# A new order of all operations in a two-layer attention and MLP kernel on one core

## The chip, the cores and the metric

The kernel runs on 1 core of one Trainium2 chip. The metric is the time of one execution on the device, in microseconds (us). The core has five engines with an instruction queue each: TensorE (PE; its weight loads are listed as PEld), VectorE (DVE), ScalarE (ACT), GpSimd (POOL) and SyncE (SP, which here only issues DMAs). Each engine works through its own queue in order; between engines, semaphores make an instruction wait for its inputs and for its buffers.

## The reference

A causal decoder trunk of two layers on 256 tokens of width 1024, in float32. Layer 0 mixes tokens with block-sparse attention of 16 heads, whose one block of 256 tokens covers the sequence, layer 1 with a dilated sliding-window attention of 12 heads in three groups. Each mixer is followed by an MLP of width 4096 with a squared ReLU, and each of the four parts by a layer norm:

```python
for i in range(DEPTH):                                   # DEPTH = 2
    mix = moba_attention(h, ...) if i % 2 == 0 else dilated_attention(h, ...)
    h = layer_norm(DEEPNORM_ALPHA * h + mix, ln_mix_g[i], ln_mix_b[i])
    h = layer_norm(DEEPNORM_ALPHA * h + sq_relu_mlp(h, w_in[i], w_out[i]), ...)

def sq_relu_mlp(x, w_in, w_out):
    return jnp.square(jax.nn.relu(x @ w_in)) @ w_out
```

## The kernel before

The function `tile_trunk` does not issue instructions as it goes. It records 3550 operations in a `Plan`: each with its engine, the function that issues it, and the operations that must come before it because of what it reads and writes. Then `Plan.emit` issues them in the order that the table `ORDER` (from line 236) gives. `ORDER` holds differences: its running sums are the numbers of the operations. Every engine's queue is that one list, cut down to the engine's own operations; so the table sets the order on TensorE, VectorE, ScalarE, POOL and SP all at once.

```python
ops = [self.ops[n] for n in itertools.accumulate(ORDER)]
```

The buffers rotate: tiles of one tag (`raw` 8 of them, `whi` 9, `wlo` 10, `ta` 6, and four PSUM banks each for `tp` and `acc`) are handed out in the order of the list, the one that came free first going first. A tile's first operation waits for the last operation on the tile that had the place before it. So a new order also changes which tile follows which.

The products are done with float32 numbers split into two parts: `split` makes the upper part on ScalarE (L433, `whi<-raw`) and the remainder on VectorE (L438, `wlo<-raw,whi`), and TensorE multiplies the parts (L443, three matmuls for one product). Weights come by DMA in pieces of 512 KB, issued on SP (`load_w`). Activations are transposed on TensorE by a product with the identity (L945).

The MLP's second product uses a scheme with seven block products instead of eight, for which sums of weight blocks are needed. `load_left` and `load_right` (L720 to L760) load two tiles and form these sums. Some are done by `add_by_dma` (L706): two accumulating DMAs of half a tile each, issued on POOL (L712). Each takes one of the three tiles named `ring`, so that a fourth has to wait until the one three before it has landed; and each waits for the `split` of the tile it adds to, whose VectorE part is the last to be done. Since POOL's queue is in order, what stands behind a waiting half waits too. The sum is then read by a VectorE add of two tiles in `raw` (L804, `raw<-raw,raw`) and by the next `split`.

In the MLP's first product, the two halves of a PSUM bank are added by `halves_sum`: ScalarE copies one half out of the bank (L1185) and VectorE adds the other to it (L804, `ta<-tp,ta`). That add is the last reader of the bank and gives it back to TensorE.

The operation numbers that the prediction speaks of:

- 2812 and 2817: the VectorE part of the splits that gate the halves of the tiles raw_952 (2813, 2814) and raw_957 (2818, 2819); 2835: the VectorE add that reads raw_952's sum.
- 1177 and 1182: the same for raw_385 (1178, 1179) and raw_388 (1183, 1184); 1241: the VectorE add that reads raw_385's sum.

Of the kernel before, what the change touches and what calls it, by code (L numbers as in the profile page):

```python
# [136 lines left out]
class Plan:  # L137
# [109 lines left out]
    8, 1, 60, -59, -74, 308, -233, 1, -75, 391, -315, 1, 1, -85, 86, 4, -3, -59, 1, 112, -103, 104, 1, 1, -53, 1, 1,  # L247
    -54, 1, 105, -104, 1, 1, 1, 1, 43, 92, -179, 47, 41, 94, -136, 90, 44, -41, 6, 39, -38, 1, 9, 1, 1, -65, -92,
    184, -79, -58, 1, 1, 59, 2, -4, 6, 6, -2, -66, 70, -67, 56, 4, -6, 4, 11, -8, 152, -149, -2, 6, -2, 191, -259,
    131, 85, -140, 4, -7, 1, 5, -4, -3, 190, -261, 76, 183, -182, 18, -54, 92, -91, 1, 63, -62, 1, 89, -27, 1, -12,  # L250
    13, -12, 13, -64, 52, 37, -88, 89, -37, 38, 1, -38, 1, 1, 9, 1, 1, 34, 1, 1, -101, 1, 1, 100, -36, -63, 64, 1,
    1, 1, 33, 1, 1, 1, 21, -123, 111, -42, -2, 98, -41, -37, 40, 1, -178, 162, 98, -44, -215, 117, 2, 250, 3, 64, 9,
    6, -73, -3, 67, -305, 1, 1, 1, 1, 33, 1, 195, -154, -74, 1, 9, 1, 64, -63, 1, 1, 1, 1, 60, -59, 60, -41, -16, 1,
    1, 207, -206, 22, 4, -6, 12, -2, -6, -6, -63, 72, -6, -5, 1, 6, -4, 6, -24, 33, -6, 10, -1, -1, -5, 2, -4, 10,
    -4, -21, 258, -61, -209, 212, 60, -231, -2, -26, 25, 2, -86, 256, -208, -1, 52, 4, 1, -4, 1, 1, 3, 1, 1, 1, 1,
    1, 1, 1, 1, 1, 1, 24, -23, 3, 21, -20, 1, 20, -24, 5, 1, 19, -18, -6, 25, 1, 1, 38, -58, 21, 9, 1, 1, 1, 1, -12,
    -21, 22, 12, -11, 12, 1, 25, -2, -35, 1, -24, 57, -55, 59, -139, 137, -15, 81, 70, -192, -2, 3, -81, 122, -40,
    127, -107, 1, 1, 106, 1, -98, 1, 1, 1, 1, 1, 1, 1, 19, -16, 1, 79, -45, -18, 141, -12, -115, -29, 2, 21, 4, -8,
    -18, 30, -6, -9, -11, 16, 3, -4, -17, 31, -17, 9, -20, 26, -4, 2, -8, -18, 3, 135, -102, -5, 1, -18, 23, 104,
    -103, 60, 1, -16, 1, 1, 1, 1, 1, 1, 1, 1, 1, 1, 7, -6, 7, 1, 1, 1, -62, 53, 10, 1, 1, 53, -52, 1, -13, 66, -52,  # L260
    1, -58, -6, -4, 6, -4, -12, 24, -22, 16, 4, -21, 5, 15, -6, -2, 4, -6, 15, -19, 72, 7, -61, 2, 1, 2, -1, -6, -4,
    12, 1, 2, 1, -2, 51, -2, 6, -8, -16, 23, -4, -2, 11, -2, 3, -2, -6, 4, 24, 7, -9, 3, 1, 6, 229, -226, 1, -3, 1,
    49, 6, 1, 1, -5, 6, -53, 2, -36, 37, 6, 29, -6, -44, -21, 81, -3, -72, -2, 18, -21, 65, -23, 1, -7, 1, 49, -85,
    29, -26, 2, -4, 85, -6, -3, -40, 1, 1, 7, 1, -4, 103, 324, -315, 104, -3, -104, 98, -206, 1, 20, 1, 1, 1, 2, 1,
    1, -24, 1, 1, 1, 2, 5, -6, 2, 5, 49, 1, -54, 18, 1, -18, 31, -27, 1, 86, 9, 95, -194, 53, 1, -23, 1, 1, 1, 21,
    1, 7, -5, -1, 2, -54, 30, 1, 1, 1, 1, 1, 24, -4, -19, 154, -134, 35, -34, 29, 106, 1, -101, -55, 1, 1, 21, -20,
    23, 1, 1, -4, -20, 1, 70, -46, 1, 1, 1, 1, 43, -70, 19, -18, 1, 50, -24, 1, 1, 41, 1, -41, 42, 1, -42, 1, 44, 1,
    -34, 1, 34, 1, 1, -20, 21, 1, 1, -50, 1, 213, 3, 100, -102, 117, -330, 116, 100, -215, 38, 1, 25, 1, -40, 1, 46,
    -45, 1, 38, 1, 6, 1, -6, 1, 1, 5, 1, -5, -42, 65, -17, 1, 1, -49, 88, -22, 234, -117, -204, 107, 235, -256, 121,
    -185, 25, -55, 15, 1, 1, 79, -95, 96, 217, -216, -80, 38, -37, 1, 37, 1, 1, -38, 1, 25, 13, 59, -71, 13, -12,  # L270
    71, 99, 116, -115, 127, -29, -102, -98, -116, 48, 12, -11, 1, 69, -68, 69, 1, 1, 1, 1, -72, 45, 1, 2, -1, 120,
    94, -212, -22, 1, 22, 1, -26, 240, -176, 8, -7, 1, 1, -66, 26, 214, 31, -268, 1, 133, -132, 3, -2, 1, 131, 112,
    61, -21, -218, -5, -12, 18, -17, 1, 1, 1, 1, 14, -13, 1, 6, 7, 1, 11, -10, -8, 9, 10, 1, -42, 1, 1, 1, 1, 39, 1,
    -39, 1, 1, 16, 22, 1, -14, 1, 15, 1, -2, 9, -94, 242, 5, -246, 94, 153, -5, 16, -31, -1, -120, 153, -152, 126,
    -2, -230, 131, 1, -62, 1, 62, 1, -48, -14, 1, 14, -13, 61, -60, 61, -48, 1, 1, 47, 1, 25, 1, 1, -26, 27, 1, 1,
    -28, 1, 1, -51, 3, 186, -173, 124, -136, 138, 30, -167, 12, -11, -96, 99, 181, -134, 1, 1, 20, 1, -61, 1, -9,
    94, -84, -13, 16, 150, -149, 81, -84, 4, -3, -14, 3, 41, 1, 11, -10, 5, 1, 1, 1, -7, 25, 1, 1, -17, 18, -20, 21,
    -18, 1, 1, 1, 1, 1, 25, 95, -94, 61, -70, 104, -107, 4, -3, 4, -3, 123, -67, 27, -144, 80, 105, -67, -46, 1, -8,
    68, -67, 1, 1, 6, -5, 56, 1, 5, -1, -49, 64, -70, 1, 91, -90, 14, 2, 1, -2, -91, -15, 96, -95, 201, -2, 1, -19,
    -13, 14, 1, 1, 1, 1, -36, 37, 1, 1, 1, -21, 22, 1, 1, -42, -3, 1, 59, -37, -24, 62, -48, 2, -1, 11, -9, 46, 1,  # L280
    -17, -86, 1, 56, 37, 10, -116, 14, 85, 8, 1, -93, 155, -61, 1, 61, 1, -171, 16, -14, 108, 6, -41, 71, 1, 1, -31,
    1, -41, -4, 46, 82, 1, 2, -187, 186, 2, 88, -87, -191, 192, -206, 119, 1, 1, 1, 1, 1, 1, 1, 73, -32, -40, 1, 1,
    37, -36, 14, 74, -149, -1, 174, -21, 79, -169, 112, -241, 205, 15, -218, 14, 114, 112, -111, 75, 39, -244, 14,
    231, -25, 32, 34, -80, 102, -163, 1, 1, 1, 1, 1, 1, 61, -60, 1, 1, 1, 1, 1, 1, -18, 19, 1, 51, 3, -53, 92, -11,
    4, -115, 123, -11, -81, 6, 1, 1, 1, 1, 1, 1, 1, 1, 1, 1, 1, 1, 36, -35, 1, 1, 30, 85, 1, -115, 1, 1, 21, -75,
    55, -171, 117, -131, 206, -20, -53, 56, 99, -101, 58, -26, 1, 1, 1, 1, 1, 1, 1, 1, 1, 1, 1, 1, 1, 1, 1, -19, 20,
    -45, 117, -22, -94, -3, 98, -50, 17, 1, 1, 1, 1, 1, 1, 1, 1, 1, 1, 1, 1, 1, 1, 1, -76, 77, -135, 155, 2, -21, 1,
    1, -79, -61, 4, 172, -35, -136, 155, -16, 109, 1, -112, 113, -97, -7, -37, 63, 1, -62, 57, 6, 1, 1, 1, 1, -68,
    81, -12, 1, -68, 78, -9, 1, 1, 1, 1, 1, 1, -42, -1, 50, -32, -1, 2, -23, 55, -31, -93, -1, 118, -32, 95, 47,
    -101, 1, 1, 1, 1, 1, 1, -10, 11, 49, -57, -55, 64, 1, -49, 69, -34, 15, 45, -25, -38, -51, 27, 130, -67, 68,  # L290
    -42, -25, -21, 1, 1, 1, 96, 79, -125, 43, -92, 48, -35, -12, -71, 72, 1, 40, -39, 46, -119, -145, 299, -80, 39,
    -89, -1, 54, -2, 81, 1, -81, 2, 1, 41, -33, 29, -28, 1, 25, -24, 1, 1, 1, 1, 1, 1, 1, 1, 1, 1, 49, -48, 1, 13,
    35, 1, 19, 52, -27, -92, 62, 79, -164, 91, 75, -80, -8, 87, -164, 167, -144, 145, -77, 75, -79, -1, -46, 1, 1,
    1, 1, 1, 1, 65, 67, -131, 1, 1, 1, 38, -37, 1, 1, 1, 56, -55, 57, 64, -63, -57, 22, 3, 61, -85, 1, 1, 20, 3, 61,
    26, -109, 55, 102, -156, 2, 53, 54, -106, 1, 106, 43, 4, 60, -98, 119, -73, -134, 1, 1, 1, 1, 81, -80, 1, 42,
    -41, 1, 1, 1, 1, 1, 1, 1, 1, 32, 72, -103, 107, -43, 47, -38, 35, -154, 4, 155, -1, -47, -106, 155, -40, -3,
    -62, 1, 1, 1, 1, 1, 1, 1, 1, 1, 87, 35, -121, 1, 1, 1, 1, 1, 93, -13, 82, -43, -118, 146, 2, -54, 53, -52, 55,
    -149, -25, 175, -140, 1, 1, 1, 1, 1, 1, 1, 1, 1, 1, 1, 1, 1, 1, 92, -91, 88, 42, -40, -89, 135, -72, -88, 150,
    15, -164, 1, 145, -58, 72, -135, -23, 148, -103, 1, 1, 1, 1, 1, 1, 1, 1, 1, 95, -94, 95, -94, 1, 1, 1, 1, 78, 1,
    -102, -1, 132, -107, 110, -109, 101, 6, -106, 28, 1, 1, 1, 1, 1, 1, 1, 56, -55, 1, 52, -51, 1, 53, -91, 39, 1,  # L300
    1, 1, 53, 27, -72, 73, -80, 9, 37, -36, 1, 1, 1, 1, 43, -42, 48, -105, 108, -107, 2, 106, -2, -105, 108, -106,
    2, 105, -106, 2, 107, 35, -23, 14, 45, -54, -29, 25, 16, 3, -96, 73, -6, -4, -55, 1, 1, 55, -54, 55, -54, 1, 70,
    -90, 91, -2, -4, -64, 1, 1, 46, 32, 1, -78, 1, 68, 5, 1, -7, -11, 14, -69, 1, 1, 1, 75, 39, -47, -2, 11, 39, 1,
    87, -84, 3, 84, -47, 138, -274, 34, -29, 18, 38, -4, 1, 1, -29, 32, -7, 39, -88, 18, 73, 3, -44, 39, 3, -38, 5,
# [1399 lines left out]
```

## Time and profile before

| what | value |
|---|---|
| runs of the kernel before | 545.91, 546.32, 546.64 us; median 546.32 |
| the profiled execution | 546.45 us |
| its span, from the first to the last instruction | 544.7 us |
| granted TensorE clock, mean | 0.998 |
| bytes moved by DMA | 115.07 MB, 211 GB/s on average |
| DMA queue q1 (SP's loads) | 101.46 MB, 54.2% of 16 engines' span |
| DMA queue q0 (POOL's halves) | 9.44 MB, 10.2% |

The profile is of one execution. A row of its timeline has the start, the length, the engine, the line, the operation, what it writes and reads, and how many instructions stand in the row; in brackets is the idle time of the engine just before it and what ended that. A row of the chain has a start, a length and an engine with a line: it follows the work back from the end, at each step to what released it. A row of the waits has the engine and line that waited, what for, the us in total, the times and the longest. A row of the DMA issues ends with KB each and the us from issue to landing.

### The profile page before, as it was taken

How to read it: one execution, taken by the hardware profiler on the slowest of the kernel's cores; microseconds unless marked ns; L12 is line 12 of the kernel's file. 1: busy time of each engine (PE TensorE's matmuls, PEld its weight loads, DVE VectorE, ACT ScalarE, POOL GpSimd, SP SyncE). 2: the span in 40 equal slices, each digit the busy share in tenths (PEclk: the TensorE clock that was granted, in tenths of full speed). 3: DMA queues.
4: the chain of work that ended last, by engine and by line, in shares of the span. 5: the costliest groups of instructions: out<-in, count | busy, mean ns of one | idle time of the engine just before them, and what ended most of it. 6: DMA issues, size and time to landing. Idle time of an engine off the chain costs nothing.

```text
span 544.7 us, 8746 instructions
## 1 busy us (share of the span) xinstructions
PE 536.1 (98%) x3157; PEld 455.1 (84%) x3157; DVE 506.9 (93%) x893; ACT 367.3 (67%) x586; POOL 38.2 (7%) x51
## 2 busy tenths in 40 slices
PE   9999999999999999999999999999999999999994
PEld 7988888888888888888888988888888888888884
DVE  6789997998999999999999899899899999999997
ACT  6549768357777878787715647827767787788820
POOL 0000000000301011110000000000110210011001
PEclk9999999999999999999999999999999999999999
DMA  8995324817778688987874655154966787799512
GB/s 332 389 394 194 116 92 147 305 45 255 216 180 216 243 199 235 262 239 275 292 262 138 248 194 194 64 208 140 281 169 193 169 246 237 257 239 263 205 39 78
DMA packets 33164, 115.07 MB, mean 211 GB/s; under 512 B 3936, under 2 KB 4832, under 8 KB 33120
## 3 DMA queue, kind: packets, MB, share of 16 engines
q1 hardware_dynamic: 28800, 101.46, 54.2%
q0 software_dynamic: 2880, 9.44, 10.2%
q10 hardware_dynamic: 1440, 3.61, 2.0%
q8 instruction: 25, 0.41, 0.3%
q14 instruction: 19, 0.16, 0.1%
HBM read 113.44 MB, written 1.05 MB: 210 GB/s over the span
## 4 chain that ended last, share of the span: by engine, by line
PE 95%; DMA 2%; DVE 1%; issue 0%; DVEq 0%; POOL 0%; ACT 0%
PE acc L443 62%; PE tp L443 31%; PE tp L945 3%; DMA raw<-in_wout_dram 1%; DMA raw<-in_xw_dram 1%; DVE tok L811 0%; DVE raw L804 0%; DVE bst L1087 0%; DVE ta L804 0%; POOL raw L712 0%; DVEq L1698 0%; DVE raw L479 0%; DVE v L438 0%; ACT xs L433 0%; DVE bst L1090 0%
## 5 line engine op out<-in xcount | busy, mean ns | idle before, releaser
L438 DVE TENSOR_TENSOR wlo<-raw,whi 128x1024 fp32r<-128x1024 f32 (+2 forms) x234 | 260.0, 1142 | 8.9 <-ACT whi L433 8.2
L433 ACT ACTIVATE whi<-raw 128x1024 fp32r<-128x1024 f32 (+2 forms) x232 | 220.9, 996 | 26.2 <-PE tp L443 8.5
L443 PE MATMUL acc<-xs,whi 128*128 128x512 f32 (+1 forms) x528 | 133.2, 374 | 0.4 <-ACT xs L433 0.3
L443 PEld LDWEIGHTS acc<-xs,whi 128*128 128x128 f32 x528 | 93.3, 189 | 18.4 <-ACT xs L433 1.2
L443 PE MATMUL acc<-xs,wlo 128*128 128x256 f32 x480 | 79.2, 282 | 0.0
L443 PEld LDWEIGHTS acc<-xs,wlo 128*128 128x128 f32 x480 | 72.4, 189 | 7.3
L443 PE MATMUL tp<-xs,whi 128*128 128x512 f32 x192 | 54.5, 394 | 0.5 <-DVE ta L804 0.5
L712 POOL DMA_DIRECT2D raw<-in_wout_dram x36 | 29.9, 968 | 218.1 <-DVE ta L804 79.3
L443 PE MATMUL acc<-whi,ahi 128*128 128x512 f32 (+1 forms) x112 | 43.2, 395 | 0.0
L443 PE MATMUL acc<-wlo,ahi 128*128 128x512 f32 (+1 forms) x100 | 38.8, 388 | 0.0
L443 PEld LDWEIGHTS tp<-xs,whi 128*128 128x128 f32 x192 | 33.4, 188 | 5.7 <-DVE ta L804 0.9
L1281 ACT ACTIVATE ta<-acc 128x512 f32<-128x512 f32 x32 | 19.0, 595 | 23.3 <-PE acc L443 23.2
L443 PE MATMUL tp<-xs,wlo 128*128 128x256 f32 x192 | 33.9, 282 | 0.0
L443 PE MATMUL acc<-whi,alo 128*128 128x512 f32 (+1 forms) x92 | 33.7, 388 | 0.0
L443 PEld LDWEIGHTS tp<-xs,wlo 128*128 128x128 f32 x192 | 30.5, 189 | 3.9
L443 PE MATMUL acc<-whi,xs 128*128 128x512 f32 (+1 forms) x112 | 30.6, 366 | 0.0
L433 ACT ACTIVATE xs<-tp 128x512 fp32r<-128x512 f32 x12 | 7.2, 596 | 33.6 <-PE tp L945 33.4
L931 ACT ACTIVATE sc<-sc,mx 128x128 f32<-128x128 f32 (+2 forms) x40 | 19.9, 501 | 10.7 <-DVE mx L921 10.6
L443 PE MATMUL tp<-whi,xs 128*128 128x512 f32 x80 | 26.1, 400 | 0.0
L1064 POOL TENSOR_TENSOR rstd<-rstd,expo 128x1 f32<-128x1 f32 x7 | 6.3, 898 | 274.1 <-DVE rstd L1062 274.1
L804 DVE TENSOR_TENSOR ta<-ta 128x128 f32<-128x128 f32 (+1 forms) x74 | 24.2, 336 | 0.8 <-ACT ta L1281 0.4
L443 PEld LDWEIGHTS acc<-whi,ahi 128*128 128x128 f32 x112 | 21.1, 188 | 4.2 <-issue 0.3
(244 smaller groups left out, 949.5 us busy)
## 6 DMA issues: line engine op xcount, KB each, us to landing
raw<-in_win_dram SPq DMA_DIRECT2D x64, 512.0 KB, 4.8
raw<-in_wout_dram SPq DMA_DIRECT2D x64, 512.0 KB, 5.3
raw<-in_wqk_dram SPq DMA_DIRECT2D x22, 512.0 KB, 6.9
raw<-in_wout_dram POOLq DMA_DIRECT2D x36, 256.0 KB, 6.7
raw<-in_wo_dram SPq DMA_DIRECT2D x14, 512.0 KB, 3.3
raw<-in_wv_dram SPq DMA_DIRECT2D x8, 512.0 KB, 5.5
raw<-in_wv1a_dram SPq DMA_DIRECT2D x4, 512.0 KB, 5.3
tok<-in_xw_dram SPq DMA_DIRECT2D x2, 512.0 KB, 7.3
```

The costliest lines, as they stand in the source:

```text
L433: a = op("ACT", act(n, sbuf=sbuf), lambda: nc.scalar.activation(hi(), src(), AF.Copy), r, whi)
L438: lambda: nc.vector.tensor_tensor(lo(), src(), f32(hi()), op=ALU.subtract), list(r) + list(whi), wlo,
L443: nc.tensor.matmul(out_ap, lhsT, rhs, start=start, stop=stop)
L712: "POOL", ADD_ISSUE, lambda rows=rows: nc.gpsimd.dma_start(dst()[rows], src()[rows], accum_op=ALU.add),
L804: op("DVE", dve(n) + extra, lambda: nc.vector.tensor_tensor(out_ap(), a(), b(), op=alu), r, w)
L931: lambda: nc.scalar.activation(e(), e(), AF.Exp, bias=bias(), scale=-1.0, accum_out=total()), r, w,
L945: nc.tensor.transpose(ps.t[:, c : c + P], src(), ident.t)
L1064: op("POOL", 0.98, lambda: nc.gpsimd.tensor_tensor(rs.t[:, 1:2], rs.t[:, 0:1], expo.t, op=ALU.pow), [(rs, 0), expo], [(rs, 1)])
L1281: op("ACT", act(512), lambda: nc.scalar.activation(w.t, ps.t, AF.Copy), [ps], [w])
```

## The change

The table `ORDER` gets other numbers from its line 247 on (the 281st operation of the list); the operations, the buffers, the first 280 entries and the last 22 are the same. No other line of the kernel differs.

```diff
@@ -244,124 +244,125 @@
     1, -21, 262, -240, 39, 7, -9, -33, 1, 1, 1, 35, -34, 1, 1, 37, -7, 203, -195, -29, 30, 60, -137, 312, -234, -7,
-    8, 1, 60, -59, -74, 308, -233, 1, -75, 391, -315, 1, 1, -85, 86, 4, -3, -59, 1, 112, -103, 104, 1, 1, -53, 1, 1,
-    -54, 1, 105, -104, 1, 1, 1, 1, 43, 92, -179, 47, 41, 94, -136, 90, 44, -41, 6, 39, -38, 1, 9, 1, 1, -65, -92,
...
-    1, 1, 3, -2, -21, 2, 24, -27, 28, -3, 1, -22, 25, -44, 5, 5, 35, 1, 1, 5, -3, -32, 31, 7, 1, 1, 1, 1, 2, 1, 1,
-    1, -4, -7, 16, -19, 20, 4, -3, 2, -1, -7, 1, 1, 1, 7, -24, 3, 22, 1, 2, -1, 2, 7, -4, 2, -4, 7, -6, 2, 2,
+    8, 1, 60, -59, -52, 53, 1, -53, 61, -52, 53, -52, 44, -43, 1, 1, 42, 1, -78, -1, -6, 47, 90, -136, 1, 41, 98, 1,
+    -98, 1, 104, -6, 1, -58, 1, 58, 1, 1, 1, -60, 4, -44, 132, -91, 94, 85, -219, 91, -90, 131, -130, 1, 133, 1,
...
+    -16, 24, -4, 5, -4, 1, 1, -21, -1, 25, 1, -36, 12, 1, 24, 1, -24, 25, 1, 1, 1, 5, -3, -1, 2, -40, 45, 1, 1, 1,
+    1, 2, 1, 1, 1, -4, 9, 1, -17, 18, 3, -1, -1, -7, 1, 1, 1, 7, -24, 3, 22, 1, 2, -1, 2, 7, -4, 2, -4, 7, -6, 2, 2,
 )
```

Taken as running sums, the two tables differ like this. A place counts as changed where another operation stands there; the shift is how many places an operation moves on its engine's queue.

| engine | operations | places changed | largest shift |
|---|---|---|---|
| PE | 1911 | 1437 | 53 |
| ACT | 555 | 460 | 54 |
| DVE | 837 | 641 | 33 |
| POOL | 47 | 23 | 2 |
| SP | 200 | 150 | 12 |

The first operation that moves ran at about 29.6 us in the profiled execution. On TensorE, the list goes from matmuls to transposes 25 times instead of 26. At the two places that the prediction takes up:

| queue | before | after |
|---|---|---|
| POOL near 396 us | 2814, 2818, 2813, 2819 | 2813, 2814, 2819, 2818 |
| POOL near 150 us | 1178, 1179, 1184, 1183 | 1178, 1183, 1179, 1184 |
| DVE, gate 2812 | place 607 | place 595 |
| DVE, gate 2817 | place 612 | place 626 |
| DVE, reader 2835 | place 627 | place 628 |
| DVE, gate 1177 | place 239 | place 240 |
| DVE, gate 1182 | place 238 | place 248 |
| DVE, reader 1241 | place 272 | place 263 |

229 rows, old and new, of the table ORDER are left out of this document.

## The prediction

> **What bounds the kernel now.** I read the page's busy line first, then the chain that ended last, then the waits of TensorE and of its weight loads, then the chain and the timelines at the one place where TensorE stood.
>
> ```profile
> span 544.7 us, 8746 instructions
> PE 536.1 (98%) x3157; PEld 455.1 (84%) x3157; DVE 506.9 (93%) x893; ACT 367.3 (67%) x586; POOL 38.2 (7%) x51
> PE 95%; DMA 2%; DVE 1%; issue 0%; DVEq 0%; POOL 0%; ACT 0%
> ```
>
> TensorE is busy for 536.1 of 544.7 us and carries 95% of the chain. A new order cannot shorten its work, which is the same 3157 matmuls; it can only close holes between them or open new ones. 544.7 − 536.1 leaves 8.6 us, and most of that is no wait inside the run. What TensorE waited for by name is little:
>
> ```profile
> PE tp L443 <- PEq L1689: 0.8, 1, 0.8
> PE tp L443 <- DVE ta L804: 0.5, 1, 0.5
> PE acc L443 <- ACT xs L433: 0.3, 1, 0.3
> ```
>
> The first and third lie in the beginning, which stays. After the last matmul the layer norm runs alone, from 536.36 us on:
>
> ```profile
> 536.36 0.70 DVE tok L811
> ```
>
> 544.7 − 536.36 is 8.3 us, and both tables end in the same 22 entries: nothing of it moves. So one named wait is open to the change, the 0.5 us on VectorE's add at L804. The timeline of TensorE and the chain around it show what it cost and why:
>
> ```profile
> 406.33 1.09 PE L443 MATMUL tp<-xs,whi 128*128 128x512 f32 x4
> 407.90 0.50 PE L443 MATMUL tp<-xs,whi 128*128 128x512 f32 x1 [0.47 <-DVE ta L804]
> 408.24 0.65 PE L443 MATMUL tp<-xs,wlo 128*128 128x256 f32 x4
> ```
>
> Four 512-column matmuls from 406.33, each 0.23 us after the one before (those are 1.09 us for four, the last of them 0.40 long), put the next at 407.26. It came at 407.90: 0.64 lost. The one behind it came 0.34 later and not 0.23: 0.11 more. Together 0.75 us.
>
> ```profile
> 396.42 0.54 POOL raw L712
> 396.95 7.33 DMA raw<-in_wout_dram
> 407.51 0.35 DVE ta L804
> 407.90 3.66 PE tp L443 x20
> ```
>
> ```profile
> 392.74 1.82 DVE L438 TENSOR_TENSOR wlo<-raw,whi 128x512 fp32r<-128x512 f32 x2
> 395.33 0.68 DVE L438 TENSOR_TENSOR wlo<-raw,whi 128x512 fp32r<-128x512 f32 x1
> 404.41 0.69 DVE L804 TENSOR_TENSOR raw<-raw,raw 128x512 f32<-128x512 f32 x1 [1.02 <-DMA raw<-in_wout_dram]
> ```
>
> Read backwards: the matmul waited for a PSUM bank that VectorE's add gives back at 407.86 (407.51 + 0.35). VectorE was late because its add of two weight tiles stood 1.02 us for an accumulating DMA, which took 7.33 us from 396.95. That DMA (operation 2813, the first half of tile raw_952) was free to go once its own gate was done, the first of the two splits from 392.74 (0.68 each, so by 393.5), but stood on POOL's queue behind operation 2818 (the first half of the next tile), and 2818 waited for VectorE's split of 395.33, which ended at 396.01. Without the 1.02 us the bank comes back at 406.84, which is 0.42 before the matmul asks. So the whole 0.75 us hangs on that queue.
>
> **The change part by part.** It is one edit, 1437 of 1911 PE places with other operations on them, so I go by what could move time.
>
> *1. The queue on POOL at 396 us.* The order there was 2814, 2818, 2813, 2819; it becomes 2813, 2814, 2819, 2818. The split that gates 2813 and 2814 moves 12 places up on VectorE; the durations of what it passes sum to 7.3 us. The one that gates the other pair moves 14 places down, 7.3 us. The reader of raw_952 keeps its place (+1). So 2813 goes out near 389 and 2814 near 394, as soon as one of the three ring buffers is free; the reader cannot come before 404.41 − 1.02 = 403.4. That is 9.4 us for the later half:
>
> ```profile
> DMA to landing us min/median/max: 3.6/6.7/9.2
> ```
>
> Even the longest of 36 landings fits, so the wait goes: −0.75. Late next is the other pair: its gate ends near 403.3, so its halves go out at 403.4 and 404, and their first reader is the second of two splits on ScalarE, near 414:
>
> ```profile
> 412.98 2.01 ACT L433 ACTIVATE whi<-raw 128x1024 fp32r<-128x1024 f32 x2 [0.68 <-PE acc L443]
> ```
>
> That leaves 10 us against at most 9.2; nothing waits. Bounds of the term: −0.75, and 0 if a landing stretches beyond any seen.
>
> *2. Bank returns.* VectorE has less to spare than the rest, 93% busy, so moving long splits ahead of short adds delays banks. The sharpest case is near 133 us: two splits of a full tile move ahead of an add that gives a bank back.
>
> ```profile
> 124.80 0.69 DVE L438 TENSOR_TENSOR alo<-tp,ahi 128x512 fp32r<-128x512 f32 x1 [0.99 <-ACT ahi L433]
> 130.56 1.23 DVE L438 TENSOR_TENSOR wlo<-raw,whi 128x1024 fp32r<-128x1024 f32 x1 [0.39 <-ACT whi L433]
> 132.32 0.42 DVE L804 TENSOR_TENSOR ta<-tp,ta 128x256 f32<-128x256 f32 x1
> ```
>
> ```profile
> 132.87 0.60 PE L945 MATMUL tp<-ident,ta 128*128 128x128 f32 x4
> ```
>
> The add ended at 132.74. Two splits of 1.23 us put it at up to 135.0 (net of a small operation that leaves, +2.27), and the transposes that take the bank, from 132.87, now come 1.15 us later by the matmuls put ahead of them, at 134.0: the bank is 1.0 us late. Against it, VectorE stood 0.99 and 0.39 us in these rows for ScalarE, and 0.99 of it hangs on transposes that come 2.3 us earlier on TensorE; with both filled the add is 0.4 late to 0.0. Bounds 0 and +1.0. I take +0.1, near the lower end, since the idle rows stand directly ahead of it and a single operation's delay is often taken up by the one behind.
>
> *3. Switches.* TensorE goes from matmuls into transposes 25 times instead of 26. One such passage:
>
> ```profile
> 88.84 0.48 PE L443 MATMUL acc<-wlo,xs 128*128 128x512 f32 x1
> 89.17 1.03 PE L945 MATMUL tp<-ident,sc 128*128 128x128 f32 x8
> 89.96 0.47 PE L443 MATMUL acc<-whi,ahi 128*128 128x512 f32 x1
> 90.27 0.39 PE L443 MATMUL acc<-wlo,ahi 128*128 128x512 f32 x1
> ```
>
> In: 0.33 from start to start and not 0.23. Out: 0.31 and not 0.23. One passage less is −0.18 us. Bounds −0.18 and 0.
>
> *4. Loads on SP.* 150 of 200 places hold another transfer, by 12 places at most. No wait of TensorE or of its weight loads is named on a load past the beginning, and counted along the two tables the shortest way from a load's issue to its first matmul is no shorter after than before. Taken as 0; if the cover went, it would cost as the 1.02 us above did, 0.74 us of TensorE per us late.
>
> *5. Weight loads.* TensorE's weight loads have named waits of their own, from 20 us on to 300 and from 300 to 520:
>
> ```profile
> PEld acc L443 <- ACT ta L1281: 0.8, 2, 0.4
> PEld tp L443 <- ACT whi L433: 0.7, 2, 0.4
> PEld tp L443 <- ACT sc L931: 0.4, 1, 0.4
> ```
>
> ```profile
> PEld tp L443 <- DVE ta L804: 0.9, 1, 0.9
> ```
>
> The last is the wait of step 1. The others, 1.9 us, are on ScalarE, whose order changes by 54 places at most. A weight load runs beside the matmul before it, so what of a 0.4 us wait reaches the matmuls is between 0 and 0.4 each. I count 0, since at none of them does a matmul show a wait; bounds −1.9 and, as new ones of that size can appear, +1.9.
>
> The Trainium skill, Perfetto Trace Analysis, section Identifying the Most-Contended Engine, calls the busy share of matmuls a poor measure, as they are pipelined, and would look at the busy share of the weight loads instead. By it the 84% of weight loads leave 89.6 us and a new order might win far more than 0.75 us; the rows with named waits above give 1.9 us at most, and the measurement decides.
>
> **Sum.** The profiled execution took 546.45 us, 1.75 more than its span, and 0.13 more than the median of the runs, 546.32 (545.91 to 546.64). 546.45 − 0.75 − 0.18 + 0.1 = 545.6.
>
> **The rivals.**
>
> *B, more is won.* If the waits of step 5 go as well, half of them gives 545.6 − 0.95 = 544.6 and all of them 543.7. For it: every engine's order is new wherever these stand. Against: a local reorder opens as easily as it closes, and no matmul shows them.
>
> *C, slower: a half on POOL is held behind another pair's gate again, now at 151 us.*
>
> ```profile
> 147.43 2.51 POOL L712 DMA_DIRECT2D raw<-in_wout_dram  x3 [6.25 <-ACT ta L1185]
> 151.30 0.81 POOL L712 DMA_DIRECT2D raw<-in_wout_dram  x1 [1.37 <-issue]
> 145.51 1.30 DVE L438 TENSOR_TENSOR wlo<-raw,whi 128x512 fp32r<-128x512 f32 x2
> 158.07 1.22 DVE L438 TENSOR_TENSOR wlo<-raw,whi 128x1024 fp32r<-128x1024 f32 x1
> 164.31 0.69 DVE L804 TENSOR_TENSOR raw<-raw,raw 128x512 f32<-128x512 f32 x1
> ```
>
> The order was 1178, 1179, 1184, 1183; it becomes 1178, 1183, 1179, 1184. The split that gates 1183 is one of the two at 145.51 and moves ten places down, 5.2 us by durations, so 1183 goes out at 151.4 and 1179, behind it, at 152.0 and not at 147.9. The reader of 1179 moves up nine places, from 164.31 to 158.9 (158.07 is the operation that stands nine places up now). From 14.4 us the room falls to 6.9. It decides above a landing of 6.9 us, where the median is 6.7. At the longest, 9.2, VectorE stands 2.3 us, and by the ratio at 407.90 (0.75 for 1.02) TensorE loses 1.7: 547.3. If all of it reaches TensorE, 2.3: 547.9. Against it: a VectorE add has other returns behind it with room, and landings vary with the load:
>
> ```profile
> q1 hardware_dynamic: 294, 1.07, 75.5%
> raw<-in_wout_dram POOLq DMA_DIRECT2D x3, 256.0 KB, 7.2
> q1 hardware_dynamic: 12, 0.04, 4.2%
> raw<-in_wout_dram POOLq DMA_DIRECT2D x1, 256.0 KB, 4.0
> ```
>
> These are the DMAs of 394 to 398 us and of 400 to 403: with SP's queue at 75.5% a half took 7.2 us, at 4.2% it took 4.0. At 7.2, the wait is 0.3 us and costs 0.2. The Trainium skill, DMA: Bandwidth & Descriptors, section Queues, rings and completion order, has each DMA engine take turns between its queues; by that rule the half at 152 us slows as far as SP's loads are busy beside it, and the two windows agree with it.
>
> *D, nothing changes.* The stall of 407.90 is one landing in one execution. If other executions don't have it, or an equal one arises elsewhere, the time stays at 546.3. For it: a landing of 6.3 us and not 7.33 would have hidden it, and half of all landings are under 6.7. Against: the three runs lie within 0.73 us.
>
> **How the numbers follow.** What a measurement can tell from no change is about 0.2%, here 1.09 us: faster means under 545.23, slower over 547.41. The forecast (its own range 545.2 to 546.0) has 0.47: its cause is seen link by link, but its size is inside the border. B has 0.21, since the waits exist but not on the matmuls; C 0.17, as the median landing just fits, with the costlier new bank returns of step 2 (+1.0, 546.5) on the same side; D 0.15. B and a sliver of the forecast end under 545.23: faster 0.23. C lies partly over 547.41 (9.2 us in full) and a larger part inside: slower 0.12. Same is the rest, 0.65. The range leaves out the far half of B and the far end of C: 544.7 to 547.3.
>
> **What would show it.** Step 1: no wait of TensorE for VectorE's add near 408, the add of raw_952 without idle time for a DMA, POOL's halves there in the new order. Step 2: an idle row ahead of transposes near 134. Step 3: 25 passages. Step 5: the list of weight-load waits shorter or with new names. C: idle time on VectorE for a DMA near 159 and TensorE standing within 3 us. The prediction is wrong if a wait longer than 1 us appears on TensorE, above all for a load whose issue moved down on SP, or if the spacing of its matmuls changes where nobody waits.

## The result: slower by 0.6%, with the predicted wait gone and two others in its place

The changed kernel takes 549.67 us (median of 6 runs, 548.12 to 551.01) against 546.29 (545.91 to 546.64): a ratio of 1.006, 95% interval 1.0041 to 1.0078. The forecast was 545.6 and the range ended at 547.3; both missed. The runs also lie further apart than before, 2.9 us against 0.73, and the profiled execution, 548.12 us, is the fastest of them. So its trace shows the least of what went wrong, and other executions have to be looked at too.

From the page of the changed kernel (its lines lie one further down than before, L444 is the old L443):

```profile
span 546.4 us, 8741 instructions
PE 536.8 (98%) x3157; PEld 455.6 (83%) x3157; DVE 506.9 (93%) x893; ACT 367.9 (67%) x586; POOL 38.6 (7%) x51
PE 88%; DVE 5%; DMA 4%; issue 1%; ACT 1%; DVEq 0%; POOL 0%; ACTq 0%
```

The work is the same. The chain has changed: 4% of it is now DMAs and 5% VectorE, where it was 2% and 1%, and TensorE has 88% and not 95%. The waits of TensorE (what waited, what for, us in all, times, longest):

```profile
PE tp L444 <- DVE ta L805: 1.7, 1, 1.7
PE tp L444 <- PEq L1690: 0.8, 1, 0.8
PE acc L444 <- ACT ta L1282: 0.2, 1, 0.2
```

The second lies in the beginning, as before. The first is a wait for an add of the same line, which gives a bank back, but 7 us earlier and with another cause. The chain there (start, us, what):

```profile
387.63 10.00 DMA raw<-in_wout_dram
...
399.62 0.51 ACT v L434
400.12 0.28 ACT ta L1186
400.40 0.02 issue
400.42 0.44 DVE ta L805
400.86 0.04 issue
400.90 3.17 PE tp L444 x15
```

and ScalarE's timeline:

```profile
397.70 2.01 ACT L434 ACTIVATE whi<-raw 128x1024 fp32r<-128x1024 f32 x2 [2.44 <-DMA raw<-in_wout_dram]
```

Backwards from TensorE: the bank came with VectorE's add of 400.42, that waited for ScalarE's copy out of PSUM at 400.12, and the copy stood on ScalarE's queue behind the split of a weight tile that began at 397.70, 2.44 us after ScalarE was free. The tile is raw_945. Its load, operation 2801 on SP, went out at 387.63 and landed 10.00 us later. Matched matmul by matmul with the order, TensorE lost 1.86 us there.

A second place, in the chain near 186 us:

```profile
175.16 0.54 POOL raw L713
175.69 7.80 DMA raw<-in_wout_dram
183.60 1.06 ACT whi L434
184.66 0.49 ACT ta L1282
185.20 0.97 PE acc L444 x3
```

```profile
183.60 1.06 ACT L434 ACTIVATE whi<-raw 128x1024 fp32r<-128x1024 f32 x1 [1.43 <-DMA raw<-in_wout_dram]
```

Operation 1207, a half on POOL, went out at 175.69 and landed 7.80 us later; ScalarE's split that reads its sum stood 1.43 us for it, ScalarE's copy out of a PSUM bank stood behind that split, and TensorE, which waited for that bank (the third row of the waits), lost 0.34 us.

The predicted part is there as well: POOL's halves 2813 and 2814, now in this order and earlier than before (396.95 and 394.06), and the add 2835, which had stood 1.02 us for one of them.

```profile
385.97 0.81 POOL L713 DMA_DIRECT2D raw<-in_wout_dram  x1 [0.87 <-ACT whi L434]
390.30 0.82 POOL L713 DMA_DIRECT2D raw<-in_wout_dram  x1 [3.53 <-issue]
406.25 0.69 DVE L805 TENSOR_TENSOR raw<-raw,raw 128x512 f32<-128x512 f32 x1
```

No idle time stands before the add, and TensorE doesn't wait at 408. In sum: −0.75 + 1.86 + 0.34 = +1.45, against 548.12 − 546.45 = +1.67 between the two profiled executions; 0.2 us is left over.

### The profile page after: what moved, and what is told of

Its sections match the earlier page's. It is cut to its first block, busy times and chain, and to the rows that moved or that the text cites. A ratio compares the mean times of both kernels' runs of the same rounds, so it can differ in the third digit from the quotient of the medians.

```text
span 546.4 us, 8741 instructions
## 1 busy us (share of the span) xinstructions
PE 536.8 (98%) x3157; PEld 455.6 (83%) x3157; DVE 506.9 (93%) x893; ACT 367.9 (67%) x586; POOL 38.6 (7%) x51
## 4 chain that ended last, share of the span: by engine, by line
PE 88%; DVE 5%; DMA 4%; issue 1%; ACT 1%; DVEq 0%; POOL 0%; ACTq 0%
PE acc L444 59%; PE tp L444 26%; DMA raw<-in_wout_dram 4%; DVE wlo L439 3%; PE tp L946 2%; DVE tok L812 1%; DVE ta L805 1%; ACT whi L434 0%; DVE xs L439 0%; DVE bst L1088 0%; DVE bst L1118 0%; ACT ta L1186 0%; DVE raw L805 0%; DVE ta L812 0%; POOL raw L713 0%
## 5 line engine op out<-in xcount | busy, mean ns | idle before, releaser
L444 PE MATMUL acc<-xs,whi 128*128 128x512 f32 (+1 forms) x528 | 132.5, 375 | 0.2 <-ACT ta L1282 0.2
L444 PEld LDWEIGHTS acc<-xs,whi 128*128 128x128 f32 x528 | 92.9, 190 | 17.6 <-ACT ta L1282 1.4
L444 PE MATMUL acc<-xs,wlo 128*128 128x256 f32 x480 | 81.8, 282 | 0.0
L444 PEld LDWEIGHTS acc<-xs,wlo 128*128 128x128 f32 x480 | 73.4, 190 | 8.1
L444 PE MATMUL tp<-xs,whi 128*128 128x512 f32 x192 | 54.6, 395 | 1.7 <-DVE ta L805 1.7
L444 PE MATMUL acc<-whi,ahi 128*128 128x512 f32 (+1 forms) x112 | 43.2, 396 | 0.0
L444 PEld LDWEIGHTS tp<-xs,whi 128*128 128x128 f32 x192 | 33.8, 188 | 7.3 <-DVE ta L805 1.9
L444 PE MATMUL acc<-wlo,ahi 128*128 128x512 f32 (+1 forms) x100 | 38.8, 388 | 0.0
L444 PE MATMUL tp<-xs,wlo 128*128 128x256 f32 x192 | 33.8, 281 | 0.0
L444 PE MATMUL acc<-whi,alo 128*128 128x512 f32 (+1 forms) x92 | 33.7, 388 | 0.0
L444 PEld LDWEIGHTS tp<-xs,wlo 128*128 128x128 f32 x192 | 30.1, 189 | 3.6
L444 PE MATMUL acc<-whi,xs 128*128 128x512 f32 (+1 forms) x112 | 30.8, 367 | 0.0
L932 ACT ACTIVATE sc<-sc,mx 128x128 f32<-128x128 f32 (+2 forms) x40 | 19.9, 500 | 12.2 <-DVE mx L922 12.1
L444 PE MATMUL tp<-whi,xs 128*128 128x512 f32 x80 | 26.6, 400 | 0.0
L444 PEld LDWEIGHTS acc<-whi,ahi 128*128 128x128 f32 x112 | 21.1, 188 | 4.2 <-issue 0.3
L805 DVE TENSOR_TENSOR ta<-ta,ta 128x128 f32<-128x128 f32 (+1 forms) x60 | 22.5, 380 | 0.2
```

The source lines that it names most:

```text
L444: nc.tensor.matmul(out_ap, lhsT, rhs, start=start, stop=stop)
L805: op("DVE", dve(n) + extra, lambda: nc.vector.tensor_tensor(out_ap(), a(), b(), op=alu), r, w)
L932: lambda: nc.scalar.activation(e(), e(), AF.Exp, bias=bias(), scale=-1.0, accum_out=total()), r, w,
```

## The experiments

All of them are the same operations in another order. An edit is told as the order on the queue concerned. A ratio is taken to runs of the kernel before beside that experiment; their medians are 546.07 to 546.32 us. Theory L at the start: the one late load 2801 makes the loss. Theory M: several transfers have little room now.

**1. The changed kernel again.** No edit.

> The changed kernel once more, for another profiled execution of it; nothing is left out. Theory L (the loss is the one weight load 2801, which went out on SP at 387.63 instead of 383.09 us and whose landing, 10.00 us later, held ScalarE): 548 to 551 us again, the profile has TensorE waiting 1 to 4 us near 401 us for VectorE's add at L805, and the slower the execution the longer that one wait. Theory M (several transfers have little room, each execution has others late): 548 to 551 as well, but the profile has waits at other places too, together over 1 us, ahead of 300 us above all (a half on POOL landed just too late at 183.5 us in the first profile and cost 0.34).

Measured: 550.28 us (548.36 to 551.09), ratio 1.0077 (1.0061 to 1.0094). The profiled execution, 551.09 us, is the slowest of its runs:

```profile
PE tp L444 <- DVE ta L805: 2.3, 1, 2.3
PE acc L444 <- ACT ta L1282: 1.2, 1, 1.2
388.41 10.57 DMA raw<-in_wout_dram
```

The load took 10.57 us this time and TensorE lost 2.43; the half on POOL landed 0.7 us later than in the first profile and cost 1.36 and not 0.34. Both places vary with the landing. There is a third item. The windows of both executions just behind the wait (stretch, us, then busy time and instructions of PE, PEld, DVE, ACT and POOL, granted clock, DMA share, GB/s), the repeated execution first and the first profile second:

```profile
402.20:406.50 4.30, 4.24 (x14) 3.55 (x15) 4.30 (x11) 1.01 (x2) 0.00 (x0) 0.63 0.00 2
```

```profile
402.20:406.50 4.30, 4.30 (x26) 3.72 (x25) 4.30 (x10) 2.06 (x4) 0.10 (x1) 1.00 0.01 2
```

TensorE is busy in both, but does 14 matmuls and not 26, at a granted clock of 0.63. That costs 4.30 × (1 − 0.63) = 1.6 us. 2.43 + 1.36 + 1.6 − 0.75 = 4.6, and 551.09 − 546.45 = 4.64. So this execution is accounted for to within a few tenths; executions differ by as much in their beginning alone (26 us in, TensorE is 0.3 us earlier here than in the profile of before). Theory M holds so far, in that there are two places.

**2. The load put back.**

```diff
-SP near 384 us: 2702, 2851, 2830, 2801, 2815
+SP near 384 us: 2702, 2801, 2830, 2851, 2815
```

> The changed order with one pair of loads exchanged: 2801 goes out where 2851 stood (near 384.2 us, 11 us ahead of its reader instead of 7.6) and 2851 where 2801 stood (near 387.6, 11 us ahead of its own reader). Theory L: the wait of TensorE near 401 us goes and with it all of the loss, 545.5 to 546.3 us. Theory M: 1.9 us go, from 549.7 to about 547.8; what remains over 546.3 lies in waits elsewhere.

Measured: 546.82 us (546.38 to 549.66), 1.002 (1.0008 to 1.0031): 3.5 us under the run beside it, more than the 1.9 of the first profile, which fits executions with a longer wait at 401 and a lowered clock behind it, as in experiment 1. The profile has no wait near 401 any more. What remains past the beginning is the second place, 1.0 us by name and 1.13 by the matmuls:

```profile
PE acc L443 <- ACT ta L1281: 1.0, 1, 1.0
```

Both theories missed the time: L by 0.5 us too low, M by 1.0 too high.

**3 and 4. Half of the new order.** The first 1700 entries (to about 243 us) from one table, the rest from the other.

> The new order for its first 1700 operations (to about 243 us), then the remaining operations in the order of before. Theory L: the load 2801 stands as before, so 546.0 to 546.6 us, and the stall of 0.75 us at 408 is there. Theory M: 547.0 to 549 us, with waits of TensorE between 150 and 245 us on what a late transfer feeds.

> The order of before for the first 1700 operations (to about 243 us), then the remaining operations in the new order. Theory L: the whole loss is here, 548.5 to 550.5 us, with TensorE waiting near 401 us. Theory M: about 547.5 us, 1.1 over before (1.86 lost at 401, 0.75 won at 408), and the rest of the loss is in the kernel with the new first half.

Measured: new first half 548.26 us, 1.0042 (1.0026 to 1.0058), with the wait near 186 (1.86 us of TensorE in this execution) and the old stall near 408; new second half 549.95, 1.0074 (1.0061 to 1.0086), with the wait at 401 to 403 (2.38 us) and nothing at 408. Each has a wait at the seam that neither table has (0.85 and 1.57 us near 245), so the two don't add up, and M's 547.5 for the second half is missed by 2.4 us. What they show is the places: both halves lose, against L.

**5. Both put back.** As 2, and:

```diff
-DVE near 173 us: 1361, 1205, 1343
+DVE near 173 us: 1205, 1361, 1343
```

1205 is the split that gates the halves 1206 and 1207; 1361, the split of another tile ahead of it, had made it wait.

> The changed order with the loads 2801 and 2851 exchanged, and with VectorE's split 1205 exchanged with the split 1361 just ahead of it, so that the halves 1206 and 1207 on POOL go out 2.0 us earlier (173.1 and 173.7 instead of 175.2 and 175.7). Theory of two places (the loss is the load 2801 and the half 1207 and nothing else): no wait of TensorE for ScalarE near 186 nor for VectorE near 401; 545.4 to 546.0 us, what the prediction gave, since the stall of before at 408 stays away. Rival (a new order has little room everywhere, and a mended place only uncovers the next): 546.3 us or more, with a wait over 0.5 us at a third place.

Measured: 545.48 us (545.08 to 545.93 in 12 runs), 0.9988 (0.9978 to 0.9997). The profile's list of TensorE's waits is down to one, that of the beginning:

```profile
PE tp L443 <- PEq L1689: 0.8, 1, 0.8
```

Two exchanged pairs out of 3550 operations give back the whole loss, and the time is that of the forecast. No third place shows. The second place has little room even so: the halves went out at 173.98 and 174.52, 1.2 us earlier and not 2.0, and 1207 landed at 182.17, 0.14 us before ScalarE came to its split at 182.31.

**6. The split alone put back.**

> The changed order with the splits 1205 and 1361 exchanged alone; the load 2801 stays late. Two places: the wait near 186 goes, that near 401 stays (1.9 to 2.5 us, more where the granted clock falls behind it): 548.2 to 549.5 us, 1 us under the changed kernel. Rival: what the first place gives back is lost again at 401, so that the time stays at 549.5 to 550.3.

Measured: 548.36 us (546.97 to 551.27), 1.0046 (1.0032 to 1.006). That is inside what two places gave, so the second place's gain isn't lost at 401. Against experiment 5, leaving the load late costs 0.0058 of the time, leaving the split late (experiment 2) 0.0032, and both, in the changed kernel, 0.0072 and 0.0089 in its two measurements. Within their intervals the two losses add up. The profiled execution is the slowest: the load took 11.62 us, TensorE lost 3.47 us at 401.62, and its clock fell to 0.50.

**7. Step 1 of the prediction alone, in the order of before.**

```diff
-POOL near 396 us: 2814, 2818, 2813, 2819
+POOL near 396 us: 2814, 2813, 2818, 2819
```

> The order of before with two operations on POOL exchanged, 2813 and 2818, so that it is 2814, 2813, 2818, 2819: step 1 of the prediction alone. Two places, and the step as predicted: the wait at 408 goes, 0.75 us less than before, 545.4 to 545.6 us. Rival: the landing of 2814 or the ring buffers hold the reader as before, or the wait moves to the next transfer: 546.0 to 546.4 us.

Measured: 545.54 us (545.17 to 546.86), 0.9993 (0.9985 to 1.0001). The wait at 408 is gone from the profile, whose execution took 545.63 and lists no wait of TensorE but that of the beginning. The gain, 0.5 us by medians, is of the size forecast, but its interval just takes in no change.

**8. The load one place earlier.** As 6, and:

```diff
-SP near 386 us: 2851, 2830, 2801, 2815
+SP near 386 us: 2851, 2801, 2830, 2815
```

> As the kernel with the splits exchanged alone, and the load 2801 one place earlier on SP, exchanged with 2830: it goes out near 386.5 us, 8.8 us ahead of its reader's unhindered start, instead of 387.6 and 7.6. Two places with a landing of 10 us whenever it goes out here: 1.14 us less waiting at 401, the rest of 0.7 to 1.3 us stays and the clock isn't lowered behind it: 546.5 to 547.2 us. Rival (the landing is 10 us only because of what goes out beside it, and one place more or less decides it): the landing is 8 us or less, no wait is left, 545.4 to 546.0.

Measured: 546.62 us (545.8 to 549.07), 1.0014 (1.0002 to 1.0026). The median is that of the first theory, but the profile, of one of the faster executions, has no wait: the load landed after 7.6 us. So neither expectation is the whole. The 12 runs reach from 545.8 to 549.07, which suggests that at this place it depends on the execution whether the load is late at all; only the one profile shows a landing.

**9. The halves moved away from the load.** As 6, with the load left in its late place, and VectorE's split 2812 thirteen places later, so that the halves 2813 and 2814 go out at 395.6 and 396.1 and not at 385 and 390.

```diff
-DVE near 384 us: 2563, 2812, 2698, 2701 ... 2485, 2704, 2582
+DVE near 384 us: 2563, 2698, 2701 ... 2485, 2704, 2812, 2582
```

> As the kernel with the splits 1205 and 1361 exchanged alone (the load 2801 stays in its late place), and VectorE's split 2812 thirteen places later on its queue, so that its two halves on POOL (2813, 2814) go out near 394 us and not at 385 and 390, beside the load 2801. Theory of crowding (the load takes 10 to 11.6 us because accumulating halves that the new order put there are in flight beside it): its landing takes 8 us or less, the wait near 401 is under 0.5 us or gone, 545.4 to 546.6 us. Rival (the load takes as long because of SP's own loads one behind the other): the landing still takes 9.5 us or more and the wait stays, 547.8 to 548.6 us.

Measured: 545.66 us (545.14 to 546.19), 0.999 (0.9981 to 0.9999). The wait is gone with the load still in its late place. Below, the two queues' shares of 384 to 397 us and the median landing of SP's loads there: first with the halves beside the load (experiment 6), then with the halves moved away.

```profile
q1 hardware_dynamic: 630, 2.29, 51.2%
q0 software_dynamic: 297, 1.02, 45.2%
raw<-in_wout_dram SPq DMA_DIRECT2D x4, 512.0 KB, 10.0
```

```profile
q1 hardware_dynamic: 881, 3.19, 67.7%
q0 software_dynamic: 160, 0.52, 25.0%
raw<-in_wout_dram SPq DMA_DIRECT2D x4, 512.0 KB, 7.2
```

With POOL's queue (q0) at 45% of the DMA engines' time SP's (q1) moves 2.29 MB in these 13 us, with 25% it moves 3.19. All 11 runs of this experiment lie below all 12 of experiment 6, so the gain is not that of one execution. Four cells for the one load 2801, from the DMA issues of its own moment, each from one profiled execution:

| | halves 2813, 2814 early (about 385, 390 us) | halves late (from 394 us) |
|---|---|---|
| load early (383 to 384 us) | 9.6 us, hidden (experiment 5) | 6.2 us, hidden (experiment 7) |
| load late (386 to 387 us) | 11.6 us, TensorE waits (experiment 6) | 7.9 us, just fits (experiment 9) |

The lower row is the one that differs by this edit alone. Its 11.6 us are of the slowest execution of experiment 6, and the two profiles of the changed kernel have 10.0 and 10.6, so the early halves go with a landing that is 2.1 to 3.7 us longer. The upper row compares two whole orders, in which SP's loads differ too. And the halves don't set the landing alone: in experiment 8 they are early as well and the load, which went out at 386.06 with one load fewer ahead of it, took 7.6 us; what made that execution's landing so short isn't shown. With both the late load and the early halves the order loses; experiments 5 and 9 each take one of the two away. The early halves are the very move that took the wait at 408 away.

**10. The load later still.** As 6, and the load exchanged with 2815 behind it.

```diff
-SP near 387 us: 2801, 2815
+SP near 387 us: 2815, 2801
```

> As the kernel with the splits 1205 and 1361 exchanged alone, and the load 2801 one place later on SP, exchanged with 2815: it goes out near 389.0 us instead of 386.7. Size: each us that the load is later reaches TensorE in full, so the wait near 401 grows by about 2.3 us, to 4.2 to 5.8. Clock: after a wait of 1.86 and one of 2.38 us the granted clock stayed at 1.00, after 2.43 and 3.47 it fell to 0.5 for some 3 us. If a wait this long always lowers it, the profile has 0.5 behind it and every execution is slow, 551.5 to 554 us; if the fall has to do with something else, the clock stays and the time is 550 to 551.

Measured: 550.61 us (548.28 to 552.09 in 4 runs), 1.0078 (1.0055 to 1.0102). The size was wrong: the load went out at 389.87, 3.2 us later than in experiment 6, but took 9.0 us and not 11.6 and landed at 398.9, only 0.5 us later. TensorE lost 3.14 us in the profiled execution. The comparison is with the slowest execution of experiment 6; against the changed kernel's two profiles the load went out 1.5 and 2.2 us later and landed 0.1 us earlier and 1.2 us later. So here a later issue didn't reach the landing in full. What sets the landing isn't shown. The clock fell again:

```profile
402.20:406.50 4.30, 4.30 (x14) 3.54 (x15) 4.30 (x10) 0.71 (x2) 0.00 (x0) 0.60 0.01 2
```

## Why the prediction was wrong

- **What bounds, and the stall at 408: right.** Step 1's chain of causes held. The changed kernel has no wait there, and experiment 7 removes it with one exchange on POOL. Rival D, that the stall is of one execution, isn't borne out: experiment 3, which has the old order there, stood 1.0 us at it. The halves went out 3 to 4 us earlier than worked out (385.97 and 390.30, not 389 and 394). That was luck, and it helped: the "longest of 36 landings", 9.2 us, was no bound, since one half took 10.1 us in experiment 5.
- **Step 4, the loads on SP: the step that failed.** "Taken as 0", because the way from a load's issue to its first matmul was no shorter. But a load's first reader is ScalarE's split, and ScalarE's queue is in order: between them the room of load 2801 fell from 12.2 us (383.09 to 395.32 in the trace of before) to 7.6 (387.63 to where ScalarE was free, 395.26). In the order of before the load landed after 5.9 us. The step used neither the room to that reader nor a landing that could change, and it didn't name ScalarE's copy, queued behind the split, on which the bank's return hangs. The term put at 0 measured 1.86 us in the first profile and 2.43 in the second. The text's own sign of being wrong, a wait over 1 us for a load whose issue moved down on SP, is what came.
- **Step 4's price: agreed by luck.** 0.74 of TensorE per us late was foreseen, and 1.86 for 2.44 is 0.76. But ScalarE stood 2.44, 2.98, 3.02, 3.73 and 4.06 us for this load in five profiles (the changed kernel, experiments 4, 1, 10 and 6), and TensorE lost 1.86, 2.38, 2.43, 3.14 and 3.47: each time 0.6 less. So 0.6 us of it is covered here, and the rest is lost in full. At the second place 1.1 us is covered: ScalarE stood 1.43, 2.23, 2.46 and 2.96 us (the changed kernel, experiments 2, 1 and 3), TensorE lost 0.34, 1.13, 1.36 and 1.86.
- **Step 1's missing half.** It counted what the earlier halves win and not what they collide with. The trace of before had shown that a half lands later beside SP's loads (7.2 us against 4.0), and the prediction used it for the halves alone, not for a load beside halves. The Trainium skill, DMA: Bandwidth & Descriptors, section Queues, rings and completion order, which it cited, has each DMA engine take turns between its queues, so a load shares the engines with halves as a half does with loads. The lower row of the table in experiment 9 agrees with it: 7.9 us against 10.0 to 11.6; the 7.6 us of experiment 8 don't.
- **Rival C: the right kind of wait, at another pair and from another cause.** At 151 us the half 1179 went out at 151.95, as worked out, and its reader at 158.33 did not wait. (Its old room was 16.4 us, 164.31 − 147.9, and not 14.4.) A half did come too late 24 us further on: VectorE's split 1205 moved 13 places down (275 to 288), its halves went out at 175.2 instead of 168.3, and ScalarE was free for their reader at 182.2, where it had come at 185.3 before. It cost 0.34 to 1.86 us in the four profiles that have it. The prediction looked for halves that stand behind another pair's gate and not for a gate that moves by itself.
- **Steps 2 and 3.** The transposes near 134 started at 133.96, as estimated, with no idle time: 0 and not +0.1. The 0.18 us of one passage fewer can't be told apart in these runs.
- **Step 5 and rival B.** Those waits of weight loads changed names and gave nothing that reached the matmuls.
- **The sum.** Without the two late transfers the gain is 0.59 us (545.48 against 546.07 beside it; 0.16 to 1.20 by the interval), which agrees with −0.75 and can't tell the −0.18. That 545.48 lies so near the forecast 545.6 is in part luck, since the sum starts from a profiled execution of 546.45. Missing were the two late transfers, and the lowered clock behind the longer waits, of which the text had nothing.

## What to carry to other kernels

For each transfer that a reorder moves, take the room from its issue to the place in the queue of its first reader, whatever engine that is, and then ask what stands behind that reader. Compare it with landings at the load that the new order itself makes: a transfer moved earlier shortens one wait and can lengthen the landings beside it. A wait behind the first reader costs its length less what the queues cover, here 0.6 and 1.1 us, and not a fixed share of it. Where runs of a kernel spread more than they did, look at the slowest execution, since the fastest hides the price.

## What the hardware showed beyond that

A wait of TensorE can cost more than its length. Behind waits that cost 2.43, 3.14 and 3.47 us the granted clock fell to 0.50, for 3.41, 3.42 and 6.82 us. In the first two the fall began 1.1 and 0.5 us after TensorE took up work again, in the third 1.2 us before. Behind 1.86 us, and behind 2.38 us in experiment 4, the clock stayed at 1.00:

```profile
402.20:406.50 4.30, 3.60 (x19) 3.08 (x20) 4.08 (x9) 2.05 (x4) 0.00 (x0) 1.00 0.04 17
```

Where a wait falls matters beside its length. In all twelve traces the clock changes only at whole multiples of 3.413 us after its first rise: in experiment 1 that rise is at 3.99 us, and the fall at 403.35 is 117 such windows later. Counted by these windows, TensorE was idle for 2.27, 2.94 and 2.09 us of the one at whose end the clock fell (experiments 1, 10 and 6). The wait of 2.38 us lies across a border at 402.49 and has 1.81 us in one window, the wait of 1.86 us has 1.69, and no other window between 10 and 530 us that the clock passed at 1.00 has more than 1.41. If idle time in a window is what decides, as these three falls suggest, the border lies between 1.81 and 2.09 us; no experiment here moved a wait within its window.

The Trainium skill, TensorE: Matmul & The Clock Gate, section What's actually happening, has the clock halved after an idle window of about 3.4 us that runs freely of the work. The half clock and the window's length agree. A fall after a window with only 2.09 us of idle time isn't in that rule, and there the measurement decides.
